# A Strassen-like feed-forward on one core: all pairs of both later parts in seven products, a spare unit before each run of downs, third sums in the fifth group

## The chip, the core and the metric

The kernel runs on one core of a Trainium2 chip, and its time is device microseconds of one execution. TensorE does the matrix products, VectorE, ScalarE and GpSimd do elementwise work, and SyncE issues the loads. Each engine works through its own queue in order and waits on semaphores for operands that another engine makes. Matrix results land in PSUM banks; everything else lives in SBUF. All times below are in microseconds unless marked otherwise.

## The reference, cut to what matters

The reference is a decoder trunk of two layers on 512 tokens of width 1024. Each layer has a half-step feed-forward block, a mixer (convolution and attention) and a second half-step feed-forward block, so there are four feed-forward blocks in a run. Each has 2816 hidden features:

```python
def swiglu(h, w_gate, w_up, w_down):
    return (jax.nn.silu(h @ w_gate) * (h @ w_up)) @ w_down

x = x + 0.5 * swiglu(rms_norm(x, ffn1_norm[l]), ffn1_w_gate[l], ffn1_w_up[l], ffn1_w_down[l])
...
x = x + 0.5 * swiglu(rms_norm(x, ffn2_norm[l]), ffn2_w_gate[l], ffn2_w_up[l], ffn2_w_down[l])
```

The change touches only these four blocks.

## The kernel before, in words

**Three multiplications for one.** Weights and activations are float32. Each operand is split into a high part (a copy rounded by ScalarE) and a low part (what the rounding left, by VectorE), and a product is three matmuls: high by high, high by low, low by high.

**Parts.** The 2816 hidden features are 22 tiles of 128. A feed-forward block takes them in three parts, given by `PARTS` (L45) as first tile, number of tiles, number of pairs: five tiles without pairs, eight tiles in four pairs, nine tiles in three pairs and three tiles over. The first part is done plainly (`ffn`, L703 to L752). The other two are done in units (L378), and this is where the change is.

**Units and the seven products.** A unit computes a 2 by 2 block product by Strassen's scheme in Winograd's form: seven products of half-size blocks instead of eight. A gate/up unit (`GateUp`) computes one hidden tile: the gate and up projections are the two output blocks. Below, g2_0 to g2_7 are the second part's gate/up units and g3_0 to g3_8 the third part's. A down unit (`Down`) computes two of the eight output tiles for all tiles of a part; d2_0 to d2_3 and d3_0 to d3_3 are the second and third part's downs. In a down, two hidden tiles form a pair, and each pair adds one step to each of the seven products; a step is three matmuls with 256 columns. With four steps a product is twelve matmuls, with three it is nine. A tile that is in no pair goes into a down as plain products with 512 columns: two per tile (one for each output tile), six matmuls.

The products are named by their weights and their activations. `u2u1` by `t1`, `g1` by `b11`, `u2` by `t4`, `g2` by `b21`, `all` by `b22`, `g1u2u1` by `t2`, and `g1u1` by `t3`. The last one, the left-over product, is run by the method `rest`, called from the body of the unit that follows. A unit has two PSUM banks, four halves a, d (first bank) and b, c (second bank). `u2u1` by `t1` fills c, `u2` by `t4` goes into d, `g1` by `b11` into a, `g2` by `b21` into b, `all` by `b22` adds to c, and `g1u2u1` by `t2` writes into a again. So the halves are copied away by ScalarE in between: c at L396, a and d at L413, and a (with `t2` in it) at L433. `g1u2u1` by `t2` can't start before the copy of L413, and the left-over product can't start before the copy of L433.

**Weights.** While a unit runs, the next unit's weights are loaded into `wraw` tiles and made ready: GpSimd forms the weight sums (`sums`, L354 to L358), ScalarE the high parts (`hi`, L364), VectorE the low parts (`lo`, L368). There are four pieces: A (`u1`, `u2`, `u2u1`), B (`g1`, `g2`), D (`g1u1`, 512 wide) and C (`g1u2u1`, `all`).

**Hidden activations.** A gate/up unit ends with the addition of L485 and the silu of L486. Its left-over product runs in the next unit's body, followed by L491, L492 and L493, which finish the hidden tile. `Gated.add` then splits it into hh (high, L672) and hl (low, L677). An even tile of a pair is first held in a copy (L657), and its half is subtracted (L662) before the split; these are the activations for `b11`, `t1`, `b21` and `b22`. `b11` and `t1` read the first and the second half of the even tiles, `b21` and `b22` those of the odd tiles. So in a part of eight tiles the last step of `b21` reads the hl of the last tile.

**Sums.** From each pair, `combine` (L679) makes three combinations as soon as its odd tile is finished (for the second part's last pair from `finish`, L497, for the others a unit later, L430). These stand in L685 to L687, and it splits them: the first two together (L690 high, L692 low), which `t2` and `t3` read, and the third sums (L689 high, L691 low), which `t4` reads.

**Order.** `body` (L391) writes down the order within a unit. TensorE's order is fixed by pinning the first matmul of each product (L380). The order on VectorE and ScalarE is the scheduler's (`PIN` is False, L47): it may move an instruction away from where the code has it, by what it expects to be ready first. The order of units is made at L755 to L765. Before the downs of the second part stands one gate/up unit of the third part as a spare, so that the second part's last hidden tile can be finished beside it:

```python
for n in (*range(8, many), *range(min(many, 8)))
...
units += gates[:1] + downs + gates[1:]
```

So the units of a block are g2_0 to g2_7, g3_8, d2_0 to d2_3, g3_0 to g3_7, d3_0 to d3_3. The spare unit makes the ninth, unpaired tile, and d3_0 stands directly behind g3_7, a tile that is unpaired too. In d2_0 alone (`sums_last`, L509) `u2` by `t4` is run in the fourth place, after the left-over product of the gate/up unit; in all other units it is second. In the third part's downs three unpaired tiles go in plainly, by `plain` (L558) and `spare` (L567): the tiles 6 and 7 with weights from B and A, the ninth from D and C (`self.ninth`). In d3_0 they come late (`close`, L593 and L601), in d3_1 and d3_2 early, in d3_3 at the end. `close` adds the kept halves (L594) and adds the results to x (`into`, L581).

## Time and profile before

| | |
|---|---|
| three runs | 1775.48, 1773.82, 1774.02; median 1774.02 |
| the profiled execution | 1775.77, of which the span is 1774.0 |
| granted TensorE clock, mean | 0.999 |
| TensorE busy | 1762.0 (99%), 11869 instructions |
| VectorE busy | 1418.2 (80%), 2021 instructions |
| ScalarE busy | 996.4 (56%), 1591 instructions |
| GpSimd busy | 999.9 (56%), 665 instructions |
| moved by DMA | 177.89 MB, mean 100 GB/s |

The span is the time from the first to the last instruction on the chip. A group row of the profile reads: line, engine, operation, output and inputs by their names in the program, shape, count, then the busy time and the mean in ns of one, then the engine's idle time just before them and what ended most of it. `PEld` is the loading of weights into TensorE, `PE` the matmul itself. A row in order of time reads: start in us from the span's start, duration, engine, line, operation; in brackets the idle time before it and what ended that. In such rows the records of matmuls overlap, so that what a matmul costs is the distance of two starts.

### The profile page before, as it was taken

Reading aid. Unit: us, or ns where it says so; the run is one execution under the profiler, and the core shown is the slowest. Engines: PE = TensorE matmul, PEld = TensorE weight load, DVE = VectorE, ACT = ScalarE, POOL = GpSimd, SP = SyncE. Lnnn points to the kernel's source line nnn. Section 1 sums busy time; section 2 is a strip of 40 time slices with the busy share of each in tenths; the row PEclk is TensorE's granted clock in tenths of the full one; section 3 lists DMA queues with packets and bytes.
Section 4 is the critical chain, followed back from the end, with each engine's and each line's share of the span. In section 5 each row is a group of like instructions: output and inputs, shape, how many; then the busy total and the mean of one; then the engine's idle time right before and its main releaser. Section 6 shows DMA issues by size and latency. Waiting matters only on the chain.

```text
span 1774.0 us, 30565 instructions
## 1 busy us (share of the span) xinstructions
PE 1762.0 (99%) x11869; PEld 1624.0 (92%) x11869; DVE 1418.2 (80%) x2021; ACT 996.4 (56%) x1591; POOL 999.9 (56%) x665
## 2 busy tenths in 40 slices
PE   9999999999999999999999999999999999999999
PEld 7899999988788899999988999999887888999998
DVE  6978878868857978888778788887788588788785
ACT  6456566545844456556534665665558354565663
POOL 3176666369863156766403666653798532567661
PEclk9999999999999999999999999999999999999999
DMA  6232333332122223323332333324231232333332
GB/s 225 91 117 98 108 108 105 124 106 96 36 84 84 84 96 108 108 96 114 112 108 71 103 101 108 108 94 157 71 110 34 72 108 71 108 96 108 108 105 75
DMA packets 74226, 177.89 MB, mean 100 GB/s; under 512 B 8951, under 2 KB 30726, under 8 KB 74080
## 3 DMA queue, kind: packets, MB, share of 16 engines
q1 hardware_dynamic: 72480, 174.10, 29.9%
q8 instruction: 93, 1.52, 0.4%
q0 software_dynamic: 1312, 1.67, 0.3%
q14 instruction: 53, 0.43, 0.1%
q10 hardware_dynamic: 288, 0.16, 0.0%
HBM read 173.79 MB, written 3.42 MB: 100 GB/s over the span
## 4 chain that ended last, share of the span: by engine, by line
PE 84%; DVE 9%; issue 3%; POOL 2%; ACT 1%; DMA 1%; SPq 0%; DVEq 0%; ACTq 0%
PE ps_pair L378 44%; PE ps_pair L142 5%; PE ps_pair L141 5%; PE ps_pair L138 5%; DVE wlo L368 4%; PE ps_d L141 2%; PE ps_d L138 2%; PE ps_d L142 2%; PE ps_sc L1018 2%; PE ps_d L378 2%; PE ps_pair L894 2%; PE ps_pair L896 2%; PE ps_pair L895 2%; PE ps_out L138 1%; PE ps_out L142 1%
## 5 line engine op out<-in xcount | busy, mean ns | idle before, releaser
L368 DVE TENSOR_TENSOR wlo<-wraw,whi 128x1024 fp32r<-128x1024 f32 (+2 forms) x400 | 527.1, 1318 | 152.6 <-ACT whi L364 152.0
L364 ACT ACTIVATE whi<-wraw 128x1024 fp32r<-128x1024 f32 (+2 forms) x400 | 378.1, 948 | 312.1 <-PE ps_pair L378 135.7
L355 POOL TENSOR_TENSOR wraw<-wraw 128x512 f32<-128x512 f32 (+1 forms) x100 | 132.2, 1322 | 518.4 <-DVE wlo L368 315.3
L378 PE MATMUL ps_pair<-acth,wlo 128*128 128x256 f32 x1088 | 307.9, 283 | 0.0
L378 PE MATMUL ps_pair<-actl,whi 128*128 128x256 f32 x1088 | 307.9, 283 | 0.0
L378 PE MATMUL ps_pair<-acth,whi 128*128 128x256 f32 x1088 | 307.9, 283 | 0.0
L378 PE MATMUL ps_pair<-th,whi 128*128 128x256 f32 x816 | 232.1, 284 | 0.8
L378 PE MATMUL ps_pair<-tl,whi 128*128 128x256 f32 x816 | 230.9, 283 | 0.0
L378 PE MATMUL ps_pair<-th,wlo 128*128 128x256 f32 x816 | 230.8, 283 | 0.0
L378 PEld LDWEIGHTS ps_pair<-actl,whi 128*128 128x128 f32 x1088 | 208.9, 192 | 0.2
L378 PEld LDWEIGHTS ps_pair<-acth,whi 128*128 128x128 f32 x1088 | 208.9, 192 | 0.2
L378 PEld LDWEIGHTS ps_pair<-acth,wlo 128*128 128x128 f32 x1088 | 208.9, 192 | 0.0
L101 ACT ACTIVATE whi<-wraw 128x1024 fp32r<-128x1024 f32 (+3 forms) x124 | 122.9, 1001 | 148.9 <-PE ps_pair L141 84.7
L358 POOL TENSOR_TENSOR wraw<-wraw 128x512 f32<-128x512 f32 (+1 forms) x100 | 179.7, 1797 | 7.8
L141 PE MATMUL ps_pair<-actl,whi 128*128 128x512 f32 x448 | 174.8, 391 | 0.3 <-DVE actl L227 0.2
L138 PE MATMUL ps_pair<-acth,whi 128*128 128x512 f32 x448 | 173.9, 393 | 0.6 <-ACT whi L101 0.6
L142 PE MATMUL ps_pair<-acth,wlo 128*128 128x512 f32 x448 | 174.1, 391 | 0.0
L357 POOL TENSOR_TENSOR wraw<-wraw 128x512 f32<-128x512 f32 (+1 forms) x100 | 167.9, 1679 | 7.8
L356 POOL TENSOR_TENSOR wraw<-wraw 128x512 f32<-128x512 f32 (+1 forms) x100 | 166.5, 1665 | 7.6
L378 PEld LDWEIGHTS ps_pair<-th,whi 128*128 128x128 f32 x816 | 156.5, 192 | 2.8 <-ACT keep L433 2.4
L378 PEld LDWEIGHTS ps_pair<-tl,whi 128*128 128x128 f32 x816 | 156.6, 192 | 0.0
L378 PEld LDWEIGHTS ps_pair<-th,wlo 128*128 128x128 f32 x816 | 156.6, 192 | 0.0
(205 smaller groups left out, 4458.6 us busy)
## 6 DMA issues: line engine op xcount, KB each, us to landing
wraw<-in_gu SPq DMA_DIRECT2D x172, 512.0 KB, 3.5
wraw<-in_wqkv SPq DMA_DIRECT2D x24, 512.0 KB, 3.5
wraw<-in_wag SPq DMA_DIRECT2D x16, 512.0 KB, 3.5
wraw<-in_wout SPq DMA_DIRECT2D x16, 512.0 KB, 3.5
wraw<-in_dn SPq DMA_DIRECT2D x60, 128.0 KB, 2.9
wraw<-in_dn SPq DMA_DIRECT2D x20, 384.0 KB, 3.2
wraw<-in_dn SPq DMA_DIRECT2D x28, 256.0 KB, 2.9
wraw<-in_dn SPq DMA_DIRECT2D x20, 320.0 KB, 3.1
```

The source lines that it names most:

```text
L101: S.activation(hi, raw, AF.Copy)
L138: first = T.matmul(ps, wh, xh, start=start, stop=False)
L141: T.matmul(ps, wh, xl, start=False, stop=False)
L142: T.matmul(ps, wl, xh, start=False, stop=stop)
L355: G.tensor_tensor(d, g1, u1, op=ALU.add)
L356: G.tensor_tensor(u1, u1, u2, op=ALU.add)
L357: G.tensor_tensor(m0, u1, g1, op=ALU.add)
L358: G.tensor_tensor(m1, m0, g2, op=ALU.add)
L364: pinned(S.activation(hi[:, : self.cols[k]], self.raw[k][:, : self.cols[k]], AF.Copy), pin)
L368: pinned(V.tensor_tensor(out=lo[:, :c], in0=self.raw[k][:, :c], in1=f32(hi[:, :c]), op=ALU.subtract), pin)
L378: mm = T.matmul(ps, l, r, start=first and i == n == 0, stop=False, skip_group_check=True)
L894: T.matmul(ps[n], xh[:, t], wh, start=k == 0, stop=False)
```

## The change

It has five pieces.

1. `PARTS`: the third part's nine tiles are four pairs and one tile over, where they were three pairs and three over. Each of its downs has four steps per product, and one plain tile.
2. The order of the third part's gate/up units: tile 0 comes first and is the spare unit before d2_0, then 1 to 8. The ninth tile (n = 8) is now the last, and it stands between the last paired tile and d3_0. The third part's pairs are held and finished in other buffers (`hold`, `spot`, `part`), since tile 0 lives through the second part's downs.
3. In the first down of both parts (`q` = 0) a body of its own: `u2` by `t4` moves to the fifth place, after `g2` by `b21`, and the copy of L413 with it. All other units have `t4` second, as before.
4. `combine` makes the combinations and splits the third sums; the split of the other two (L690, L692) moves into `settle`, which is called right after for most pairs, and from the first down's body for the last pair of a part. That last pair is combined from `finish` in both parts (`soon`).
5. The ninth tile's weights for all eight output tiles are loaded once, with d3_0's weights, and split in d3_0 (`part_ninth`, 256 columns and then 768), where each down loaded and split its own two blocks within C and D.

```diff
-PARTS = ((0, 5, 0), (5, 8, 4), (13, 9, 3))
+PARTS = ((0, 5, 0), (5, 8, 4), (13, 9, 4))
...
-            if not self.sums_last:
-                self.go(self.d, "u2", "t4", first=True)
+            self.go(self.d, "u2", "t4", first=True)
...
-            if self.sums_last:
-                self.go(self.a, "g1", "b11", first=True)
             if prev:
                 prev.rest()
-            if self.sums_last:
-                self.go(self.d, "u2", "t4")
-            else:
-                self.go(self.a, "g1", "b11")
+            self.go(self.a, "g1", "b11")
...
-            self.soon = n == 2 * gated.pairs - 1 and n + 1 == gated.many
+            self.soon = n == 2 * gated.pairs - 1
...
         def combine(self):
-            self.gated.combine(self.n, self.banks[0])
+            if self.n % 2:
+                self.gated.combine(self.n, self.banks[0])
+                self.gated.settle()
...
+            self.raw = {"A": u, "B": g, "C": more, "D": d}
+            self.cols = {"A": whole * P, "B": whole * P, "C": 2 * J, "D": J}
+            if self.left and not self.q:
+                self.h.ninth = ring("wraw")
+                for m in range(KT):
+                    pull(self.h.ninth, m * P, m, whole, self.many)
...
+        def body(self, nxt, prev, prev2):
+            if self.q:
+                return super().body(nxt, prev, prev2)
+            if nxt:
+                nxt.load()
+            self.begin()
+            self.go(self.c, "u2u1", "t1", first=True)
+            pinned(S.activation(self.keep[:, 3], self.c, AF.Copy))
+            self.h.settle()
+            nxt.hi("A")
+            nxt.lo("A")
+            self.go(self.a, "g1", "b11", first=True)
+            prev.rest()
+            prev.finish(0)
+            prev.finish(1)
+            nxt.hi("D")
+            nxt.lo("D")
+            prev.finish(2)
+            self.go(self.b, "g2", "b21")
+            self.go(self.d, "u2", "t4")
+            pinned(S.activation(self.keep[:, :2], by_two(self.banks[0]), AF.Copy))
+            nxt.hi("B")
+            self.go(self.c, "all", "b22")
+            nxt.lo("B")
+            nxt.hi("C")
+            self.go(self.a, "g1u2u1", "t2")
+            pinned(S.activation(self.keep[:, 2], self.a, AF.Copy))
+            if self.left:
+                self.h.part_ninth(0, 2)
+            self.close()
+            nxt.lo("C")
+            if self.left:
+                self.h.part_ninth(2, KT)
...
         def plain(self, ps, n, first=False):
...
+            m = 2 * self.q + n
+            w = [tuple(t[:, m * P : (m + 1) * P] for t in self.h.nine)]
+            self.product(ps, zip(w, [self.h.hh[self.many - 1]]), first)
...
+        def part_ninth(self, m0, m1):
+            if not m0:
+                th = self.fp.tile([P, 6, SEQ], F32R, tag="th", name="nine")
+                self.nine = [th[:, 2 * n : 2 * n + 2, :].rearrange("p n c -> p (n c)") for n in range(2)]
+            c = slice(m0 * P, m1 * P)
+            hi, lo = (t[:, c] for t in self.nine)
+            pinned(S.activation(hi, self.ninth[:, c], AF.Copy))
+            pinned(V.tensor_tensor(lo, self.ninth[:, c], f32(hi), op=ALU.subtract))
...
             pinned(S.activation(four[:, a], last, AF.Copy))
-            pinned(S.activation(hi, t, AF.Copy))
             pinned(V.tensor_tensor(four[:, b], last, f32(four[:, a]), op=ALU.subtract))
-            pinned(V.tensor_tensor(lo, t, f32(hi), op=ALU.subtract))
             self.sums.append((hi, lo, four))
+            self.open = t, hi, lo
+
+        def settle(self):
+            if self.open:
+                t, hi, lo = self.open
+                self.open = None
+                pinned(S.activation(hi, t, AF.Copy))
+                pinned(V.tensor_tensor(lo, t, f32(hi), op=ALU.subtract))
...
-                gates = [
-                    GateUp(fp, halves, gu[m0 + n, 0], gu[m0 + n, 1], n, h)
-                    for n in (*range(8, many), *range(min(many, 8)))
-                ]
+                gates = [GateUp(fp, halves, gu[m0 + n, 0], gu[m0 + n, 1], n, h) for n in range(many)]
                 units += gates[:1] + downs + gates[1:]
```

More of the change, by code (lines that the diff above doesn't have):

```diff
@@ L415, in body @@
                 prev.finish(0)
-            if nxt and self.early_free:
+            if nxt:
                 nxt.lo("B")
@@ L572, in early @@
         def early(self):
-            if self.early_free and not self.last:
+            if self.left and not self.last:
                 self.spare()
         def middle(self):
-            if self.early_free and not self.last:
+            if self.left and not self.last:
                 self.plain(self.banks[1], 0)
@@ L587, in close @@
             two, keep = by_two(self.banks[1]), self.keep
-            late = not self.early_free or self.last
-            rest = 2 * self.steps < self.many
+            late = self.left and (self.last or not self.q)
             if self.last:
@@ L618, in rest, with one_tile, __init__, spot @@
             self.after(B)
+    def one_tile(pool, tag, dtype, name, bufs=None):
+        return pool.tile([P, SEQ], dtype, tag=tag, name=name, **({"bufs": bufs} if bufs else {}))
     class Gated:
[L622 to L625 removed]
+        def __init__(self, fp, pairs, many, ahead=False):
+            self.fp, self.pairs, self.many, self.ahead = fp, pairs, many, ahead
+            self.hh, self.sums, self.held, self.slots, self.open = {}, [], {}, [], None
+        def spot(self, n):
+            return (n - 1) % self.many if self.ahead else n
+        def hold(self, n):
+            if self.ahead and not n:
+                return const.tile([P, P + SPACE], F32, tag="ones_r", name="hold")[:, :SEQ]
+            return one_tile(self.fp, ("hh", "hl")[n // 2 % 2] + ("7" if self.ahead else "8"), F32, "hold")
         def part(self):
@@ L655, in add @@
                 if first:
-                    self.held[n] = self.fp.tile([P, SEQ], F32, tag=self.hold[n // 2 % 2], name="hold")
+                    self.held[n] = self.hold(n)
                     pinned(S.activation(self.held[n], us, AF.Copy))
```

65 lines of the change are left out of this document (21 added, 44 removed).

## Prediction

> **What bounds the kernel.** I read the page first (engines, chain), then TensorE's idle time by group, then TensorE, VectorE, ScalarE and GpSimd in order of time around the first down of the second part.
>
> ```profile
> PE 1762.0 (99%) x11869; PEld 1624.0 (92%) x11869; DVE 1418.2 (80%) x2021; ACT 996.4 (56%) x1591; POOL 999.9 (56%) x665
> ...
> PE 84%; DVE 9%; issue 3%; POOL 2%; ACT 1%; DMA 1%; SPq 0%; DVEq 0%; ACTq 0%
> ...
> L378 PEld LDWEIGHTS ps_pair<-th,whi 128*128 128x128 f32 x816 | 156.5, 192 | 2.8 <-ACT keep L433 2.4
> ```
>
> TensorE is busy 99% of the span, so a gain must come from fewer TensorE slots or from the few waits inside its stream. Those are small: 2.4 us in all behind the copy of L433, and, in the groups by shape, 2.5 us behind the third sums (L691):
>
> ```profile
> L378 PEld LDWEIGHTS ps_pair<-hs,whi 128*128 128x128 f32 x672 | 105.9, 192 | 3.5 <-DVE hs L691 2.5
> ```
>
> 2.5 us is four times 0.62: once in each of the four feed-forward blocks. What a slot costs is read from TensorE in order of time, in a last-block down:
>
> ```profile
> 1739.81 0.28 PE L378 MATMUL ps_pair<-hh,whi 128*128 128x256 f32 x1
> ...
> 1741.25 0.40 PE L378 MATMUL ps_pair<-hh,whi 128*128 128x512 f32 x1
> ...
> 1743.32 0.28 PE L378 MATMUL ps_pair<-hh,whi 128*128 128x256 f32 x1
> ```
>
> Twelve 256-wide matmuls start in 1741.25 - 1739.81 = 1.44 us (0.120 each), nine 512-wide in 2.07 us (0.230 each). The records themselves (0.28, 0.40) overlap.
>
> **The place that decides.** Below is the first down of the second part, d2_0, in the first block. Its product groups of twelve start on TensorE at 180.85 (u2u1 by t1), 182.29 (g1 by b11), 183.73 (the gate/up unit's left-over product), 185.17 (u2 by t4, the third sums) and 187.32 (g2 by b21).
>
> ```profile
> 185.17 0.40 PE L378 MATMUL ps_pair<-hs,whi 128*128 128x256 f32 x2
> ...
> 186.25 0.28 PE L378 MATMUL ps_pair<-hs,whi 128*128 128x256 f32 x1
> 186.98 0.39 PE L378 MATMUL ps_pair<-hs,whi 128*128 128x256 f32 x1 [0.44 <-DVE hs L691]
> 187.20 0.28 PE L378 MATMUL ps_pair<-hs,wlo 128*128 128x256 f32 x1
> 187.32 0.28 PE L378 MATMUL ps_pair<-hh,whi 128*128 128x256 f32 x1
> ...
> 190.19 0.28 PE L378 MATMUL ps_pair<-hs,whi 128*128 128x256 f32 x1
> ```
>
> The fourth group's eleventh matmul is due at 186.37 and starts at 186.98, 0.61 late; the next follows after 0.22 instead of 0.12, so such a hold costs 0.10 more: 0.70 in all. VectorE's queue says why:
>
> ```profile
> 180.84 2.32 DVE L368 TENSOR_TENSOR wlo<-wraw,whi 128x1024 fp32r<-128x1024 f32 x1
> ...
> 183.41 1.45 DVE L692 TENSOR_TENSOR hs<-hold,hs 128x512 fp32r<-128x512 f32 x1
> 184.78 1.21 DVE L368 TENSOR_TENSOR wlo<-wraw,whi 128x1024 fp32r<-128x1024 f32 x1
> 185.91 0.69 DVE L485 TENSOR_TENSOR ps_pair<-ps_pair,keep 128x512 f32<-128x512 f32 x1
> 186.51 0.41 DVE L691 TENSOR_TENSOR hs<-ps_pair,hs 128x256 fp32r<-128x256 f32 x1
> 186.84 0.68 DVE L677 TENSOR_TENSOR hl<-ps_pair,hh 128x512 fp32r<-128x512 f32 x1
> 187.44 0.42 DVE L491 TENSOR_TENSOR ps_pair<-ps_pair,keep 128x256 f32<-128x256 f32 x1
> 187.89 0.43 DVE L492 TENSOR_TENSOR ps_pair<-ps_pair,keep 128x256 f32<-128x256 f32 x1
> 188.24 0.68 DVE L368 TENSOR_TENSOR wlo<-wraw,whi 128x512 fp32r<-128x512 f32 x1
> 188.84 0.69 DVE L493 SCALAR_TENSOR_TENSOR ps_pair<-ps_pair,keep 128x512 f32<-128x512 f32 x1
> 189.44 1.94 DVE L368 TENSOR_TENSOR wlo<-wraw,whi 128x1024 fp32r<-128x1024 f32 x1
> 191.29 0.68 DVE L677 TENSOR_TENSOR hl<-ps_pair,hh 128x512 fp32r<-128x512 f32 x1
> 191.90 3.95 DVE L368 TENSOR_TENSOR wlo<-wraw,whi 128x1024 fp32r<-128x1024 f32 x2
> ```
>
> Without a gap come the low half of the sums (L692), two other pieces, the low half of the third sums (L691, done 186.92), and only then the low half of the last feature tile, hl (L677, done 187.52). TensorE starts 0.06 after the operand it lacks (186.92 to 186.98). b21 reads that last tile in its tenth to twelfth matmuls.
>
> **The change, part by part.**
>
> (1) Slots. In each of the third part's four downs one more pair goes into the seven products: twelve 512-wide matmuls go (12 x 0.230 = 2.76), 21 of 256 come (21 x 0.120 = 2.52). Gain 0.24 a down, 0.96 a block, 3.84 in all; the instruction count is settled by the diff. [...] The trace's slots say 3.84.
>
> (2) d2_0, u2 by t4 moved to the fifth place, g2 by b21 to the fourth. The diff means to put the sums' two parts (L690, L692) off until the down has begun. In the built order nothing of that is left: on VectorE and ScalarE the instructions and their waits are the same as before up to L491/L677 of this place, with L692 ahead of L691 and hl behind both. So VectorE's times above stand, and b21, now in the fourth place, asks at 186.37 for an hl that is done at 187.52: start 187.58, hold 1.21 + 0.10 = 1.31, where t4's was 0.70. T4 then finds its operands ready. Cost +0.61 at t2, due 190.80 instead of 190.19.
>
> (3) The copy L413 of the a and d halves now follows t4 in the fifth place, with one group (b22) instead of two until t2 overwrites a. In ScalarE's built order stand before it: the high parts of D and B, a hold copy (the next gate is now the first of a pair) and the high part of C.
>
> ```profile
> 186.63 0.60 ACT L486 ACTIVATE keep<-ps_pair 128x512 f32<-128x512 f32 x1 [1.95 <-DVE ps_pair L485]
> 187.13 1.57 ACT L364 ACTIVATE whi<-wraw 128x512 fp32r<-128x512 f32 x2
> 188.60 0.59 ACT L413 ACTIVATE keep<-ps_pair 128x512 f32<-128x512 f32 x1
> 189.56 0.60 ACT L672 ACTIVATE hh<-ps_pair 128x512 fp32r<-128x512 f32 x1 [0.38 <-DVE ps_pair L493]
> 190.06 1.05 ACT L364 ACTIVATE whi<-wraw 128x1024 fp32r<-128x1024 f32 x1
> ```
>
> Worked out: t4 runs 187.92 to 189.36, and what waits for it is released 0.22 later (last start + 0.28 + 0.06), at 189.58. The hold copy waits for L493 (189.53): 189.58 to 190.18. C's high part, 1.05: to 191.15. L413, 0.59: 191.05 to 191.64 (starts overlap by 0.1, as in the rows). t2 starts at 191.70, due 190.80: 0.90 + 0.10 = 1.00. Bounds: 0, if the copy were served right at 189.58 (190.17); 1.6, if a transfer or a sum is late by one more 0.6 copy. I take 1.00, the queue as built. d2_0 in sum: +1.61 a block.
>
> (4) The third part's gates in order 0 to 8, with n = 8 as the spare unit before d3_0, and a fourth pair. The new pair adds per block five ScalarE and eight VectorE instructions (with those of the ninth tile's weights). In the gate units they lie beside TensorE: the second part's gates do the same work with no hold but the L433 ones, which I leave as they are. But d3_0 now meets what d2_0 meets. Before it had three unpaired tiles and slack, VectorE waiting 3.00 us in its middle:
>
> ```profile
> 313.11 0.70 DVE L594 TENSOR_TENSOR ps_pair<-ps_pair,keep 128x512 f32<-128x512 f32 x1 [3.00 <-PE ps_pair L378]
> ```
>
> After the change the built order around d3_0 is that of d2_0 (L692, a weight part, L485, L691, hl), so on d2_0's clock: b21 waits for hl, +1.31 (bounds 0, if VectorE is 1.15 ahead here, and 1.7 with one more piece of 0.4 before hl).
>
> (5) d3_0's L413 stands behind two copies of the ninth tile's weights (256 and 768 wide), B, C and hh:
>
> ```profile
> L318 ACT ACTIVATE th<-ht 128x768 fp32r<-128x768 f32 x16 | 13.1, 837 | 2.3 <-DVE ht L317 2.2
> L689 ACT ACTIVATE hs<-ps_pair 128x256 fp32r<-128x256 f32 x28 | 10.7, 382 | 9.5 <-DVE ps_pair L687 9.5
> ```
>
> 187.75 + 0.38 + 0.84 less overlaps = 188.8; B to 189.8; C to 190.7; hh to 191.2; L413 to 191.72; t2 191.78, due 190.80: 0.98 + 0.10 = 1.08 (bounds as in 3).
>
> (6) d3_0's plain product follows t2. Its second matmul (due 191.78 + 1.44 + 0.10 + 0.23 = 193.55) needs hl of the ninth tile, and VectorE's built order puts before that: L491, L492, D (188.92 as above), the ninth's weights 256 wide, L493, the ninth's 768 wide, B and C.
>
> ```profile
> L319 DVE TENSOR_TENSOR tl<-ht,th 128x768 fp32r<-128x768 f32 x16 | 15.0, 950 | 0.0
> 189.00 1.29 POOL L355 TENSOR_TENSOR wraw<-wraw 128x512 f32<-128x512 f32 x1 [4.69 <-DVE wlo L368]
> 190.37 2.15 POOL L356 TENSOR_TENSOR wraw<-wraw 128x512 f32<-128x512 f32 x1
> 192.60 2.16 POOL L357 TENSOR_TENSOR wraw<-wraw 128x512 f32<-128x512 f32 x1
> ```
>
> 188.9 + 0.4 (L691's size) + 0.65 + 0.95 = 190.9; B 1.94 and C 1.97 (half of 3.95): 194.75; hl 0.6: 195.35; TensorE at 195.41: hold 1.86 + 0.10 = 1.96. The weight parts take 1.94 and 1.97 instead of 1.21 where GpSimd's sums run (rows of 189.00 on), and the same sums run here. Bounds: 0.3 with 1.21 for each; 3.6 with 2.32 for each and the ninth's parts slowed as well. I take the rows of the same stretch. [...]
>
> (7) At nothing:
>
> ```profile
> wraw<-in_dn SPq DMA_DIRECT2D x60, 128.0 KB, 2.9
> ```
>
> GpSimd's sums are 512 instead of 384 wide, by the rows of 189.00 on a quarter of 1.29 + 3 x 2.15, 1.9 more a down; cover: GpSimd is 56% busy. C is 1024 wide instead of 896, an eighth of 1.21, 0.15 more on VectorE. The ninth tile's eight loads stand in SyncE's queue ahead of d3_1's, no longer with each down; one lands 2.9 after its issue, and the unit they lie beside lasts 84 x 0.120 = 10.1. Uncovered, they would cost up to 2.9 a block. Queued behind the held matmuls is all of TensorE's stream, so holds add in full.
>
> **Sum.** Per block -0.96 + 1.61 + 1.31 + 1.08 + 1.96 = +5.00; four blocks +20.0. The profiled execution took 1775.77 (span 1774.0): 1795.8. The median shown is 1774.02, 1.75 lower: I predict 1794.0. What a measurement of this kernel tells from no change is about 0.2%, 3.5 us.
>
> **Rivals.**
> - It gets faster: the fifth place hides t4 and no other hold comes. Per block -0.96 - 0.70, so 1767.4. It decides if hl is done before 186.37, that is if VectorE has 1.15 less before it there. For it: t4 alone was late. Against: L677's row behind L691. 5%.
> - d2_0 as worked out, d3_0 without any hold, because VectorE enters the third part's gates rested: -0.96 + 1.61 = +0.65, 1776.6, no change to be told. It needs VectorE over 1.15 ahead at d3_0. Against: nine units lie between, as before d2_0. 7%.
> - Only the b21 holds: ScalarE serves L413 in time and hl of the ninth is nearly hidden: -0.96 + 0.61 + 1.31 + 0.3 = +1.26, 1779.1 (up to 1784 with one hold more). 15%.
> - All holds as worked out, between 1784 and 1803: 63%.
> - VectorE's backlog after d3_0 also reaches d3_1, or the shifted loads come late: above 1803 (1.96 raised to 3.6 gives 1800.6; loads 2.9 late in each block 1805.6). 10%.
>
> Range 1779 to 1803. Faster by over 0.2% 0.05, within 0.07, slower 0.88.
>
> **What would show it.** TensorE's group on hh and hl idle behind L677's successor, about 1.2 in d2_0 and in d3_0 of each block; the third-sum wait (L691) gone from TensorE; waits on the copy of a and d before t2, about 1; a wait of 2 on hl in d3_0's 512-wide group; 512-wide matmuls of L378 down by 192, 256-wide up by 336. I am wrong if VectorE's hl comes ahead of L692, if d3_0 starts with VectorE idle, or if the ninth tile's hl is early.

## The result, and the profile after

The changed kernel takes 1805.12 (median of six, 1802.98 to 1806.43), the kernel before, measured beside it, 1774.78 (1773.82 to 1777.25). The ratio is 1.0169, 95% interval 1.0156 to 1.0182. The profiled execution took 1805.85, its span 1803.7, 29.7 longer than the span before. The forecast was 1794.0 with a range up to 1803.0: the direction and most places were right, the time lies 2.1 above the range, and the rise is half as large again as the forecast one.

The page of the changed kernel, parts 1 and 6; a row of part 6 ends with the median us from issue to landing:

```profile
PE 1765.9 (98%) x12013; PEld 1630.7 (90%) x12013; DVE 1458.7 (81%) x2053; ACT 1007.2 (56%) x1611; POOL 1032.8 (57%) x665
...
wraw<-in_dn SPq DMA_DIRECT2D x60, 128.0 KB, 3.2
```

TensorE lost its 99%. Where it waits is in its groups by shape; the last field is the idle time ahead of the group and what ended it:

```profile
L378 PE MATMUL ps_pair<-hl,whi 128*128 128x256 f32 x512 | 146.1, 285 | 7.4 <-DVE hl L716 7.4
...
L378 PE MATMUL ps_pair<-hs,whi 128*128 128x256 f32 x704 | 132.5, 287 | 5.9 <-ACT keep L564 5.9
...
L378 PE MATMUL ps_pair<-hh,nine 128*128 128x512 f32 x32 | 13.9, 436 | 5.6 <-DVE ps_pair L608 5.6
...
L378 PE MATMUL ps_pair<-hl,nine 128*128 128x512 f32 x16 | 7.2, 450 | 8.7 <-DVE hl L716 8.7
```

Three of these are the forecast ones: b21 for hl (7.4), t2 for the copy of a and d (5.9; L564 is the copy's line in the first downs), the ninth tile's plain product for its hl (8.7). The wait on the third sums' low half (L691 before) is gone. The third row, 5.6 behind the addition of L608, was in no step of the prediction.

TensorE in order of time in block 1, at the first four of these places:

```profile
187.35 0.39 PE L378 MATMUL ps_pair<-hl,whi 128*128 128x256 f32 x1 [1.02 <-DVE hl L716]
...
191.41 0.50 PE L378 MATMUL ps_pair<-hs,whi 128*128 128x256 f32 x2 [0.70 <-ACT keep L564]
...
310.72 0.39 PE L378 MATMUL ps_pair<-hl,whi 128*128 128x256 f32 x1 [0.88 <-DVE hl L716]
...
318.95 0.50 PE L378 MATMUL ps_pair<-hl,nine 128*128 128x512 f32 x1 [2.17 <-DVE hl L716]
```

The brackets count from the modelled end of the matmul before. By the distance of starts, less the slot, the holds are 1.18, 0.86, 1.04 and 2.33 (and 0.93 at 314.85 for d3_0's copy), each with about 0.10 more at the next matmul. These are the numbers used below.

At the end of the last down, d3_3, there is a place that the prediction passed over:

```profile
354.64 0.40 PE L378 MATMUL ps_d<-hh,nine 128*128 128x512 f32 x1
...
355.11 0.39 PE L378 MATMUL ps_d<-hh,nine 128*128 128x512 f32 x1
358.03 0.80 PE L378 MATMUL ps_pair<-hh,nine 128*128 128x512 f32 x1 [2.52 <-DVE ps_pair L608]
358.62 0.63 PE L378 MATMUL ps_pair<-hl,nine 128*128 128x512 f32 x1
```

The spare product is down to three matmuls, and the next one waits for the addition of L608 (L594 before): 358.03 - 355.11 - 0.23 = 2.69. VectorE and ScalarE there, after the change:

```profile
355.54 0.70 DVE L617 TENSOR_TENSOR ps_d<-ps_d,keep 128x512 f32<-128x512 f32 x1 [0.77 <-PE ps_d L378]
356.15 1.22 DVE L102 TENSOR_TENSOR wlo<-wraw,whi 128x1024 fp32r<-128x1024 f32 x1
357.28 0.69 DVE L608 TENSOR_TENSOR ps_pair<-ps_pair,keep 128x512 f32<-128x512 f32 x1
...
354.77 1.06 ACT L101 ACTIVATE whi<-wraw 128x1024 fp32r<-128x1024 f32 x1 [1.57 <-issue]
355.74 0.36 ACT L427 ACTIVATE keep<-ps_pair 128x256 f32<-128x256 f32 x1
```

Two things are seen. The copy of a (L427) stands behind a weight part of the mixer that follows (L101). And on VectorE the spare product's subtraction and another mixer weight part (L102, 1.22) stand ahead of the addition. Before, the same place had nine spare matmuls, 2.07, in front of the addition, which came early enough:

```profile
346.00 0.38 ACT L433 ACTIVATE keep<-ps_pair 128x256 f32<-128x256 f32 x1 [1.08 <-PE ps_pair L378]
...
346.41 0.70 DVE L594 TENSOR_TENSOR ps_pair<-ps_pair,keep 128x512 f32<-128x512 f32 x1 [1.13 <-ACT keep L433]
```

Behind two kinds of hold the matmuls themselves are slow. Windows of the changed kernel; the columns are stretch, length, busy time of TensorE, its weight loads, VectorE, ScalarE and GpSimd with their instructions, granted TensorE clock, DMA share and GB/s:

```profile
317.00:319.00 2.00, 0.05 (x1) 0.06 (x1) 2.00 (x3) 1.33 (x2) 1.92 (x2) 1.00 0.74 242
...
320.50:323.80 3.30, 3.30 (x17) 3.30 (x17) 2.39 (x4) 0.38 (x1) 1.14 (x1) 0.50 0.21 78
324.00:327.00 3.00, 3.00 (x25) 2.86 (x24) 1.25 (x2) 2.35 (x4) 0.00 (x0) 1.00 0.02 5
...
358.00:361.40 3.40, 3.37 (x13) 3.09 (x14) 1.46 (x3) 0.96 (x2) 0.00 (x0) 0.51 0.48 154
```

For 3.413 after some of the long holds the granted clock is 0.50: from 320.37 on, 1.4 after d3_0's hold has ended in block 1, and from 357.92 on, just before d3_3's ends. A 256-wide matmul then takes 0.213 instead of 0.120, a 512-wide one 0.43. In this execution such a stretch stands behind d3_0's hold in block 1 and behind d3_3's in blocks 1 and 3, and costs 1.45, 1.59 and 1.42. Blocks 2 to 4 have the same hold of 2.33 or 2.34 at d3_0 with no slow stretch; the fifth experiment comes back to this.

The account of the 29.7, from starts on TensorE:

| | forecast | in the trace |
|---|---|---|
| slots | -3.84 | -3.7 |
| d2_0: b21 and t2, less t4's old wait | +6.4 | +6.2 |
| d3_0: b21 | +5.2 | +4.4 |
| d3_0: t2 | +4.3 | +4.1 |
| d3_0: plain product | +7.8 | +9.8 |
| d3_3: plain product | none | +6.2 |
| matmuls at half the clock | none | +4.5 |
| outside the units (most of it in the first mixer) | none | -1.6 |

The slots' row is what is left of the four blocks' growth (10.94, 5.17, 9.33, 5.94) when the rows under it down to the clock's are taken off; it is 0.89 to 0.98 a block. The last row is not the change's: the profiled execution of the kernel before has a stretch at clock 0.50 in its first mixer, from 494.92 on, and that of the changed kernel has none there.

### The profile page after: what moved, and what is told of

It reads as the page before. It is cut to its first block, busy times and chain, and to the rows that moved or that the text cites. A ratio compares the mean times of both kernels' runs of the same rounds, so it can differ in the third digit from the quotient of the medians.

```text
span 1803.7 us, 30881 instructions
## 1 busy us (share of the span) xinstructions
PE 1765.9 (98%) x12013; PEld 1630.7 (90%) x12013; DVE 1458.7 (81%) x2053; ACT 1007.2 (56%) x1611; POOL 1032.8 (57%) x665
## 3 DMA queue, kind: packets, MB, share of 16 engines
q8 instruction: 94, 1.54, 0.4%
## 5 line engine op out<-in xcount | busy, mean ns | idle before, releaser
L368 DVE TENSOR_TENSOR wlo<-wraw,whi 128x1024 fp32r<-128x1024 f32 (+1 forms) x400 | 549.9, 1376 | 146.3 <-ACT whi L364 145.8
L364 ACT ACTIVATE whi<-wraw 128x1024 fp32r<-128x1024 f32 (+1 forms) x400 | 380.2, 952 | 298.4 <-PE ps_pair L378 145.0
L355 POOL TENSOR_TENSOR wraw<-wraw 128x512 f32<-128x512 f32 x100 | 137.0, 1370 | 517.6 <-DVE wlo L368 290.7
L378 PE MATMUL ps_pair<-actl,whi 128*128 128x256 f32 x1120 | 317.0, 283 | 0.0
L378 PE MATMUL ps_pair<-acth,wlo 128*128 128x256 f32 x1120 | 316.9, 283 | 0.0
L378 PE MATMUL ps_pair<-acth,whi 128*128 128x256 f32 x1120 | 316.9, 283 | 0.0
L378 PEld LDWEIGHTS ps_pair<-acth,whi 128*128 128x128 f32 x1120 | 215.1, 192 | 0.2
L378 PEld LDWEIGHTS ps_pair<-actl,whi 128*128 128x128 f32 x1120 | 215.0, 192 | 0.2
L378 PEld LDWEIGHTS ps_pair<-acth,wlo 128*128 128x128 f32 x1120 | 215.0, 192 | 0.0
L101 ACT ACTIVATE whi<-wraw 128x1024 fp32r<-128x1024 f32 (+3 forms) x124 | 123.2, 1000 | 153.2 <-PE ps_pair L141 91.9
L358 POOL TENSOR_TENSOR wraw<-wraw 128x512 f32<-128x512 f32 x100 | 186.8, 1868 | 7.8
L357 POOL TENSOR_TENSOR wraw<-wraw 128x512 f32<-128x512 f32 x100 | 178.9, 1789 | 7.8
L356 POOL TENSOR_TENSOR wraw<-wraw 128x512 f32<-128x512 f32 x100 | 173.5, 1735 | 7.6
```

The costliest lines, as they stand in the source:

```text
L101: S.activation(hi, raw, AF.Copy)
L355: G.tensor_tensor(d, g1, u1, op=ALU.add)
L356: G.tensor_tensor(u1, u1, u2, op=ALU.add)
L357: G.tensor_tensor(m0, u1, g1, op=ALU.add)
L358: G.tensor_tensor(m1, m0, g2, op=ALU.add)
L364: pinned(S.activation(hi[:, : self.cols[k]], self.raw[k][:, : self.cols[k]], AF.Copy), pin)
```

## The experiments

Each is an edit of the changed kernel unless it says otherwise; `pin` keeps an instruction behind the one that the code has ahead of it on its engine. The kernel before was measured again beside them, with medians from 1774.05 to 1775.36, so the times alone don't tell differences of 1 or 2 between experiments.

**The last down's plain products early.** The argument `last` is false for d3_3 too.

```diff
-                    Down(fp, dn, m0, many, pairs, q, h, after if end else lambda m: None, end and q == KT // 2 - 1)
+                    Down(fp, dn, m0, many, pairs, q, h, after if end else lambda m: None, False)
```

> One edit to the changed kernel: the last down of the third part (d3_3) runs its two plain products early, like d3_1 and d3_2, and no longer behind the addition of L608 at its end. The changed kernel is 1805.1; its trace shows TensorE idle 2.69 at that place in blocks 1 and 3 (0.68 in block 4), and after the first two some 1.5 each of matmuls at about twice their slot. Theory A (the hold is the place's own: three matmuls of the spare product are too short a cover for the copy of a and the addition): the idle and the slow stretch go, -2 x 4.2 - 0.8 = -9.2, so 1796. Theory B (VectorE and ScalarE are late there anyway, with the next phase's weights in front): the next phase's first products wait instead, and 1803 to 1806 stays.

Measured: 1802.87, ratio to the kernel before 1.0164 (1.0149 to 1.0179): not to be told from the changed kernel. The wait on L608 is gone, and another stands a little further on:

```profile
L378 PE MATMUL ps_pair<-hs,whi 128*128 128x256 f32 x704 | 131.1, 284 | 9.1 <-ACT keep L564 5.9 <-ACT keep L427 3.2
```

The unit's own left-over product writes into a, so it waits for the copy of a (L427): 1.51 in blocks 1 and 3, 0.63 in block 4. Theory B had the place wrong (not the next phase's products) and the reason right: the copy itself is late, behind the mixer's weights. In block 4, where no mixer follows, the copy starts at once and the product still waits 0.63, because nothing stands between t2 and it. So the lateness of the copy is 1.51 - 0.63 = 0.88 of d3_3's 2.69.

**Hl ahead of the sums.**

```diff
-            self.h.settle()
+            self.h.settle(True)
...
-                pinned(S.activation(hi, t, AF.Copy))
-                pinned(V.tensor_tensor(lo, t, f32(hi), op=ALU.subtract))
+                pinned(S.activation(hi, t, AF.Copy), pin)
+                pinned(V.tensor_tensor(lo, t, f32(hi), op=ALU.subtract), pin)
```

> One edit to the changed kernel: in both first downs the split of the last pair's sums is held behind the copy of L551 (pinned in program order), so that VectorE makes the low half of the last paired tile (hl, L716) ahead of the sums' low half (L738, 1.45). Theory A (holds are single and add up): the waits on hl in d2_0 (1.18 + 0.10) and d3_0 (1.04 + 0.10) go, -4 x 2.42 = -9.7, so 1795.4. Theory B (VectorE's backlog is the limit, and the same work still stands ahead of the copies that t2 waits for): the wait on hl goes, but the copy of a and d (L564) comes at the same time as before, so that the wait at t2 grows by 0.5 to 1.2 in each; in d3_0 the plain product's wait on the ninth tile's hl grows by what is left. Then -2 to -5 in all, so 1800 to 1803.

Measured: 1796.84, 1.0124 (1.0107 to 1.0141), so 8.3 less: nearer to A. VectorE around d2_0:

```profile
182.12 1.98 DVE L368 TENSOR_TENSOR wlo<-wraw,whi 128x1024 fp32r<-128x1024 f32 x1
184.03 0.69 DVE L476 TENSOR_TENSOR ps_pair<-ps_pair,keep 128x512 f32<-128x512 f32 x1
184.62 0.41 DVE L729 TENSOR_TENSOR hs<-ps_pair,hs 128x256 fp32r<-128x256 f32 x1
184.96 0.68 DVE L716 TENSOR_TENSOR hl<-ps_pair,hh 128x512 fp32r<-128x512 f32 x1
185.56 0.68 DVE L738 TENSOR_TENSOR hs<-hold,hs 128x512 fp32r<-128x512 f32 x1
```

Hl stands ahead of the sums' low half (L738) and b21's hold is 0.11 in block 1, about 0.6 in the other three; at d3_0 it is gone. The copy's holds did not grow as B had it: 0.79 in d2_0 and 0.32 in d3_0. The ninth tile's wait stayed at 2.1 to 2.5. So the order was the cause of b21's wait in d3_0, and of half of it or more in d2_0: there the weight part that moved up in front of hl takes 1.98, where it took 1.21, and eats part of the 1.45. The waits are mostly single ones.

**The copy of a and d ahead of B and C.** In the first downs' body:

```diff
-            nxt.hi("B")
+            nxt.hi("B", True)
...
-            nxt.hi("C")
+            nxt.hi("C", True)
```

> One edit to the changed kernel: in both first downs the next down's high parts B and C are held behind the copy of a and d (L564) on ScalarE, which then follows at once on the weight part D (and, in d2_0, the hold copy). Theory A (holds add up): the waits on that copy before t2 go, 0.96 in d2_0 and 1.03 in d3_0, -8.0 in all, so 1797. Theory B (VectorE's backlog is the limit): in d2_0 the wait goes (-3.8), but in d3_0 the plain product then waits for the ninth tile's hl by as much more, so 1801.

Measured: 1795.21, 1.0115 (1.0100 to 1.0131), more than A. In d2_0 the wait is gone, in d3_0 0.26 is left of 0.93. But the edit did a second thing: with the high parts B and C later, the scheduler put their low parts behind the ninth tile's hl, and that wait (2.33) went too. In return copies in the next downs come late: d2_1's left-over product waits 0.43 for the copy of a, and d3_1's t2 0.78 for that of a and d in blocks 2 and 3. Neither theory had that; as a test of the copy alone the run is spoilt.

**The ninth tile's hl ahead of D, B and C in d3_0.**

```diff
-            nxt.hi("D")
-            nxt.lo("D")
+            nxt.hi("D", bool(self.left))
+            nxt.lo("D", bool(self.left))
...
-            nxt.lo("B")
+            nxt.lo("B", bool(self.left))
```

> One edit to the changed kernel: in d3_0 the ninth tile's hl (L716) stands ahead of the next down's low parts D, B and C on VectorE (pinned in program order), as hh does ahead of the high part D on ScalarE. My reading (1.94 + 1.97 of low parts B and C stand in front of hl): the plain product's wait of 2.33 + 0.11 goes, and the stretch of slow matmuls behind it in block 1 with it: -4 x 2.44 - 1.5 = -11.3, so 1794. Rival (the low parts are then late for d3_1, whose u2u1 by t1 and g1 by b11 wait for them): the wait is passed on to d3_1, 1800 to 1805.

Measured: 1797.10, 1.0126 (1.0111 to 1.0141), 8.0 less. The wait on the ninth tile's hl is gone in all four blocks, and d3_1 doesn't wait for its weights: the rival falls. In the trace t2's wait in d3_0 went down too, from 0.93 to 0.32, 2.5 in all that the forecast did not have. What is missing came back in other places. D3_3's hold is now 3.61 in blocks 1 and 3, with slow matmuls behind both (mean granted clock 0.996), 3.3 more: TensorE came earlier to a place where the addition comes when it comes. B21's wait in d3_0 is longer in blocks 2 to 4, 1.6 more in all; it varies from trace to trace (1.56 in block 4 of the last experiment, which leaves this place as it is). And this execution has a slow stretch in its first mixer, 1.6.

**TensorE kept busy in d3_3's hold.** `fills` is [1, 0, 1, 0], one entry for each block.

```diff
             if self.last:
                 self.spare()
+                if fills.pop(0):
+                    self.fill()
...
+        def fill(self):
+            ps = bank(("y", "tp")[self.q % 2], "ps_fill")
+            for n in range(11):
+                mm = T.matmul(ps, self.h.nine[0][:, :P], self.h.hh[8][0], start=n == 0, stop=False, skip_group_check=True)
+                tc.keep_in_program_order(mm)
```

> One addition to the changed kernel: in d3_3 of blocks 1 and 3, TensorE runs eleven more 512-wide matmuls into a bank that nobody reads, between the spare product and the one that waits for the addition of L608 (11 x 0.230 = 2.5, the hold there is 2.69). Theory A (the slow matmuls behind a long hold come from TensorE having been idle): the hold's end stays where it is, the matmuls behind it start at 0.230 and 0.120 again, and the time falls by the slow stretches of these two places, about 1.4 each where an execution has them: 1802 to 1804. Theory B (the slow stretch has another cause than the idle time): slots of about 0.43 and 0.21 stand behind the filled hold too, and 1805 stays.

Measured: 1803.50, 1.0157 (1.0140 to 1.0174). The times alone don't separate the two, the trace does. The windows of the filled place in block 1, and the matmuls behind it:

```profile
352.50:357.00 4.50, 4.48 (x26) 3.57 (x24) 3.73 (x5) 1.33 (x2) 0.16 (x1) 1.00 0.36 122
357.00:360.40 3.40, 3.40 (x21) 3.05 (x22) 2.19 (x4) 1.49 (x3) 0.59 (x5) 1.00 0.63 172
```

```profile
357.00 0.50 PE L380 MATMUL ps_pair<-hh,nine 128*128 128x512 f32 x1
357.33 0.40 PE L380 MATMUL ps_pair<-hl,nine 128*128 128x512 f32 x1
357.57 0.39 PE L380 MATMUL ps_pair<-hh,nine 128*128 128x512 f32 x1
357.80 0.40 PE L380 MATMUL ps_pair<-hs,whi 128*128 128x256 f32 x2
```

The granted clock is 1.00 and the slots are 0.23, in both filled places. So here the slow stretch follows the idle time, not the place.

Whether a hold is followed by one can be compared within the changed kernel's trace. Its slow stretches in the units last 3.413 each and start whole multiples of 3.413 apart: at 320.37, 357.92 and 1252.21, which lie 11 and 262 times 3.413 from one to the next. So this trace can be cut into stretches of 3.413 on its own grid. Four of them; a slow one follows the first three, none the fourth:

```profile
316.96:320.37 3.41, 1.42 (x7) 1.21 (x8) 3.41 (x3) 1.33 (x2) 3.25 (x3) 1.00 0.71 219
354.51:357.92 3.41, 0.99 (x6) 0.52 (x4) 2.64 (x5) 1.33 (x2) 0.00 (x0) 1.00 0.51 155
1248.80:1252.21 3.41, 1.29 (x8) 0.81 (x7) 2.65 (x4) 1.33 (x2) 0.00 (x0) 1.00 0.47 151
1211.25:1214.66 3.41, 1.59 (x13) 1.27 (x11) 3.41 (x3) 1.33 (x2) 3.33 (x2) 1.00 0.32 99
```

By the distances of starts less the slots, TensorE is idle for 2.10, 2.58, 2.29 and 1.99 in these. In the units of this trace every other stretch at full clock has 1.76 or less, and none of those is followed by a slow one. The holds of 2.33 and 2.34 in blocks 2 to 4 lie across a border of the grid (the one that ends at 1215.02 across 1214.66), and the stretch that has most of such a hold has 1.75, 1.99 and 1.76 of idle time in all. How many slow stretches an execution has differs between executions of one kernel: the mean granted clock of the changed kernel's six is 0.997 to 0.999.

**D2_0 back in its old order.** A body of its own for the second part's first down, with t4 behind the left-over product and b21 behind t4.

```diff
+            if not self.left:
+                return self.body2(nxt, prev, prev2)
...
+            self.go(self.a, "g1", "b11", first=True)
+            prev.rest()
+            self.go(self.d, "u2", "t4")
+            pinned(S.activation(self.keep[:, :2], by_two(self.banks[0]), AF.Copy))
...
+            self.go(self.b, "g2", "b21")
+            nxt.hi("C")
+            self.go(self.c, "all", "b22")
+            self.go(self.a, "g1u2u1", "t2")
```

> One part of the change undone: d2_0 alone has the order of the kernel before (t4 in the fourth place, b21 in the fifth, the copy of a and d behind them); everything else is as in the changed kernel. By the prediction's steps (2) and (3), with what the trace of the changed kernel shows: b21's wait (1.18 + 0.10) and t2's wait (0.86 + 0.10) go, t4's wait of 0.70 comes back, 4 x -1.54 = -6.2, so 1799. Rival (the waits come from the work that the new order of gates brings, not from the moved product): d2_0 keeps about 2.2 of waiting and 1804 to 1806 stays.

Measured: 1801.64, 1.0151 (1.0136 to 1.0166), 3.5 less. In the trace b21's and t2's waits are gone from d2_0, and t4's is back at 0.58 in blocks 2 to 4:

```profile
L378 PE MATMUL ps_pair<-hs,whi 128*128 128x256 f32 x704 | 132.1, 285 | 4.4 <-ACT keep L566 3.1 <-DVE hs L758 1.3
```

The waits of d2_0 belong to the moved product; the rival falls. The gain is less than 6.2 in part because this profile has slow matmuls in five places, with a mean granted clock of 0.995 (three and 0.997 in the changed kernel's).

**The code's order everywhere.**

```diff
-PIN = False
+PIN = True
```

> The changed kernel with PIN = True: VectorE and ScalarE keep the order in which the code has the units' instructions (hl ahead of the sums' low half, the copy of a and d ahead of the high part B, the sums in the first down's body as written). Theory A (the order that the scheduler chose makes the holds of the first downs): b21's, t2's and the plain product's waits go in d2_0 and d3_0, -4 x 6.85 = -27.4 at best, so 1778, and 1785 with one of them left. Theory B (VectorE has too much to do before these places in any order, and a fixed order lets other instructions wait in line): holds of the same sum stand elsewhere, 1795 or more.

Measured: 1917.83, 1.0804 (1.0788 to 1.0820). Theory B, and far beyond it:

```profile
L378 PE MATMUL ps_pair<-th,whi 128*128 128x256 f32 x816 | 241.6, 296 | 52.6 <-DVE hs L729 52.6
...
L378 PE MATMUL ps_pair<-hs,whi 128*128 128x256 f32 x704 | 138.0, 294 | 30.2 <-ACT keep L564 23.4 <-ACT keep L407 6.8
```

In the code's order the gate/up units wait for the third sums' low half of the pair just combined (L729), whose source lies in the unit's bank. The scheduler's freedom is worth far more than the places that it spoils.

**Three pins and d3_3 reordered.** The edits of "Hl ahead of the sums", "The copy ahead of B and C" and "The ninth tile's hl" together, and t2 ahead of b22 in the last down:

```diff
-            self.go(self.c, "all", "b22")
+            if nxt:
+                self.go(self.c, "all", "b22")
             self.go(self.a, "g1u2u1", "t2")
             pinned(S.activation(self.keep[:, 2], self.a, AF.Copy))
+            if not nxt:
+                self.go(self.c, "all", "b22")
```

> The changed kernel with three orders pinned in both first downs (the sums' split behind the copy of L551; the high parts B and C behind the copy of a and d; in d3_0 the ninth tile's hl ahead of the low parts D and B), and with t2 ahead of b22 in d3_3, so that twelve more matmuls cover the copy and the addition there. If the holds are single ones and add up, 6.85 - 0.7 (b21 in d2_0 stayed at 0.6 when its order alone was pinned) = 6.1 a block goes, -24.6, and in d3_3 about 1.2 in two blocks and the slow stretches, -6: 1775, the time of the kernel before. If VectorE's backlog passes them on (to d3_1's copies and to d3_3), 1783 to 1790.

Measured: 1782.67, 1.0042 (1.0027 to 1.0057), so 22.5 of the 30 are gone. That lies 7.7 above the first forecast and just below the second's range: most holds were single, and part was passed on. No slow matmuls are left in the trace's feed-forward blocks (mean granted clock 1.000), and the executions lie within 1.1 of each other where the changed kernel's lie within 3.5. What is left: 0.58 and 0.52 in d2_0, 0.36 and 0.50 in d3_0, 0.82 in d3_2 of three blocks (the copy of a and d, L407; the changed kernel has no hold there), 1.32 in d3_3 of two.

**One step of the change alone, on the kernel before.** The split of the second part's last sums pinned late, all else as before.

```diff
             pinned(S.activation(four[:, a], last, AF.Copy))
-            pinned(S.activation(hi, t, AF.Copy))
             pinned(V.tensor_tensor(four[:, b], last, f32(four[:, a]), op=ALU.subtract))
-            pinned(V.tensor_tensor(lo, t, f32(hi), op=ALU.subtract))
             self.sums.append((hi, lo, four))
+            self.open = t, hi, lo
+            if n + 1 < self.many:
+                self.settle()
...
             pinned(S.activation(self.keep[:, 3], self.c, AF.Copy))
+            if self.sums_last:
+                self.h.settle(True)
```

> The kernel before (three pairs, its order of units, t4 in the fourth place of d2_0) with one step of the change alone, and made to hold: the split of the second part's last sums is pinned behind the copy of L396 in d2_0, so that the third sums' low half (L691) and hl come 1.45 earlier on VectorE. By my reading of the first trace (L692, 1.45, stands ahead of L691, which is 0.61 late) the wait of 0.70 in each block goes: -2.8, so 1772 where the kernel before has 1774.5. Rival (another piece takes its place on VectorE, or t2 then waits for the sums): within 1 of the kernel before.

Measured: 1772.67 over eleven runs against 1774.11 over sixteen, ratio 0.9991, interval 0.9982 to 1.0000. VectorE at d2_0:

```profile
185.09 0.41 DVE L692 TENSOR_TENSOR hs<-ps_pair,hs 128x256 fp32r<-128x256 f32 x1
185.42 0.68 DVE L679 TENSOR_TENSOR hl<-ps_pair,hh 128x512 fp32r<-128x512 f32 x1
186.02 0.68 DVE L701 TENSOR_TENSOR hs<-hold,hs 128x512 fp32r<-128x512 f32 x1
```

All four waits of t4 are gone, and the four blocks' units are shorter by 0.56 to 0.59 each, 2.3 in all. In the medians 1.4 of it is seen, at the edge of what the measurement tells. Slow stretches in the mixers blur the times: the profiled execution of this kernel has two, from 493.54 and 1374.18 on (mean granted clock 0.998), that of the kernel before one (0.999). Among the executions whose mean granted clock was 1.000, this kernel took 1771.21 to 1771.88 (four) and the kernel before 1773.29 to 1774.30 (eight). It has the lowest median of this study.

**The combined kernel with d2_0 in the old order, sums late.** The three pins and d3_3's order as two experiments above, with the body that puts d2_0 back in its old order, and `settle(True)` in that too.

> The last combined kernel (1782.7) with d2_0 back in the order of the kernel before, the sums' split pinned late as there. In its trace d2_0 still had 0.58 + 0.52 + 0.20 of waiting a block. Theory A (the moved product gains nothing over the old order once the sums are late): 4 x -1.3 = -5.2, so 1777.5. Theory B (b21 or t2 waits for hl or the copy in the old order too): 1780 to 1783.

Measured: 1780.59, 1.0035 (1.0022 to 1.0048), so 2.1 less where 5.2 was expected. By the ratios it is 1.2 and the intervals overlap, so the times don't tell the two apart; the profiled spans differ by 2.9. In the trace the holds of d2_0 (1.3 a block) are gone but for 0.09, and d2_1's left-over product now waits 0.29 + 0.10 for its copy of a. That leaves about 0.8 a block. The time lies in theory B's range, but b21 and t2 don't wait: it is theory A for d2_0, with a part passed on to the next unit.

**The ninth tile's second weight piece later.** As the last, and `part_ninth(2, KT)` pinned.

```diff
-                self.h.part_ninth(2, KT)
+                self.h.part_ninth(2, KT, True)
```

> As the kernel before it in this call, and the second piece of the ninth tile's weights (768 columns) pinned behind the low part C in d3_0 on ScalarE and VectorE, so that hh and hl of the ninth tile come 0.84 and 0.95 earlier. If these pieces are what is left of the wait at d3_0's plain product (0.36 + 0.50 + 0.2 a block): -4.2 more, so 1773. If d3_1's spare product, which reads that piece, now waits for it instead: no gain, 1777 or more.

Measured: 1792.97, 1.0108 (1.0095 to 1.0122), 12 more. The wait moved on and grew:

```profile
L378 PE MATMUL ps_d<-hh,nine 128*128 128x512 f32 x32 | 14.0, 437 | 12.6 <-ACT nine L709 8.6 <-DVE nine L710 4.0
```

D3_1's spare product now waits 3.0 and then 1.3 for this piece in blocks 1 to 3, with slow matmuls behind (mean granted clock 0.995). D3_0's waits are gone, as expected, but this place is worse for the piece.

**T2 ahead of b22 in d3_3 alone.** The diff shown with the three pins, without the pins.

> The changed kernel with t2 ahead of b22 in d3_3 alone. If the hold there (2.69 in blocks 1 and 3, 0.68 in block 4) comes from a cover that shrank from nine 512-wide matmuls to three (2.07 to 0.69) in front of an addition whose operand comes late, 1.44 more of cover takes 1.2 to 1.4 off each of the two long ones, and with a hold of 1.3 the slow stretch behind it does not come: 1800 to 1803. If the addition is late by itself (its copy and the next phase's weights on ScalarE and VectorE come when they come), the hold stays above 2.

Measured: 1797.44, a single run, below the forecast. The hold is 0.33 in blocks 1, 3 and 4, where 1.3 was expected to be left. The trace has no slow stretch in its feed-forward blocks (mean granted clock 1.000), not even behind d3_0's hold of 2.34 in block 1, which the edit leaves as it is; that 1.45 is not the edit's. D3_3 in block 1:

```profile
354.00 0.39 PE L378 MATMUL ps_d<-hh,nine 128*128 128x512 f32 x1
354.56 0.50 PE L378 MATMUL ps_pair<-hh,nine 128*128 128x512 f32 x1 [0.17 <-DVE ps_pair L611]
...
352.30 0.38 ACT L428 ACTIVATE keep<-ps_pair 128x256 f32<-128x256 f32 x1 [0.20 <-PE ps_pair L378]
...
353.80 0.70 DVE L611 TENSOR_TENSOR ps_pair<-ps_pair,keep 128x512 f32<-128x512 f32 x1
```

The addition (L611 here) is done by 354.5, where TensorE needs it at 354.23. It is more than the cover: with t2 earlier, the copy (L428) also comes ahead of the second mixer weight, and the addition ahead of the spare product's subtraction. So cover and order are not told apart in blocks 1 and 3. Block 4, with no mixer behind, tells the cover: its hold in the changed kernel is 0.68. The cover shrank by six matmuls, 6 x 0.230 = 1.38, and the slack before was 0.75 (in block 4 the addition was done at 1765.33 + 0.70 and the product that needs it began at 1766.78, in block 1 at 346.41 + 0.70 and 347.86), which leaves 0.63. The other 2.0 in blocks 1 and 3 are what stands ahead of copy and addition: 0.88 by the copy behind the mixer's weight part (L101, first experiment), and 1.12 by the addition behind L617 and L102, which starts 1.54 after the copy (355.74 to 357.28) where it starts 0.42 after it in block 4 (1796.25 to 1796.67). With that order the six matmuls would have covered 1.38 of the 2.69.

## Why the prediction was wrong in size, and where it was right

**Right: the mechanism and the places.** TensorE's stream decides; the sums that the code puts off are back in front of hl in the built order; and the five terms that were costed came to 20.8 in the trace against 20.0 forecast, in part by luck, because d3_0's first two holds were 1.0 shorter in all and its last 2.0 longer. When one of them was taken away, the next hold of the same down did not grow (hl ahead of the sums); what was passed on came mostly in later units, above all in d3_3 (the ninth tile's hl: 2.69 to 3.61).

**(1) Slots.** -3.84 forecast, -3.7 in the trace. The trace's slots, 0.120 and 0.230, were the right price.

**(2), (3) D2_0.** Holds of 1.21 and 0.90 forecast, 1.18 and 0.86 measured. That L564 stands behind the hold copy and the high part C was read from the built order and was so. D2_0 in its old order took both away again.

**(4), (5) D3_0 on d2_0's clock.** 1.21 and 0.98 forecast, 0.93 to 1.04 and 0.93 measured. The rival "d3_0 without any hold because VectorE is rested" fell.

**(6) The plain product.** 1.86 forecast, 2.33 to 2.34 measured. The order was right, a size was off: the low parts B and C took 4.51 for the two, not 1.94 + 1.97, and GpSimd's sums ran beside them (three from 313.31 to 319.42):

```profile
313.78 4.51 DVE L368 TENSOR_TENSOR wlo<-wraw,whi 128x1024 fp32r<-128x1024 f32 x2
318.21 0.68 DVE L716 TENSOR_TENSOR hl<-ps_pair,hh 128x512 fp32r<-128x512 f32 x1
```

2.25 each is near the upper bound's price (2.32).

**What failed: step (1) as an all-gain, and the cover that it took away.** The prediction counted twelve 512-wide matmuls a down as gone and asked nowhere what they had covered. In d3_3 six of them stood between t2 and the product that waits for the addition of L594. Asking there what the prediction asked of the first downs (what waits, and what stands in front of it) would have shown it: the built order has L617 and L102 ahead of L608. That is +6.2 of the missing 9.7: in blocks 1 and 3, 0.67 of the 2.69 is the lost cover itself and 2.0 the order of copy and addition, which the prediction did not read there; in block 4 it is the cover alone.

**What failed: "holds add in full".** They added more than in full at three of the long ones: the slow matmuls behind holds of 2.33 to 2.69 cost 4.5 in the profiled execution. How many such stretches an execution has differs, so this part of the miss varies: the mean granted clock of the six executions is 0.997 to 0.999. The rival above 1803 named another mechanism (late loads, a backlog into d3_1), and neither was seen: d3_1 of the changed kernel has no hold above 0.2.

## What to carry to other kernels

A matmul that a change saves may have been the cover of a wait: for each removed group ask what starts behind it and how long that had been done. Where the code says that a step comes later, read it in the built order of that engine, and pin the one instruction that matters, not all of them: one pin on the kernel before took 2.3 of waiting away, all pins on the changed kernel cost 113. And keep TensorE's holds short: here three of 2.33 to 2.69 cost another 1.42 to 1.59 each, in matmuls at half the clock.

## What the runs showed of the hardware that was not expected

In the changed kernel's trace the granted TensorE clock fell to 0.50 for 3.413 after holds of 2.33 to 2.69, but not after each: 2.33 and 2.34 in blocks 2 to 4 were not followed by it. The slow stretches lie on a grid of 3.413: in the units of this trace the three stretches of the grid with 2.10, 2.29 and 2.58 of idle time were followed by a slow one, and those with 1.99 or less were not. With TensorE kept busy through the hold (fifth experiment, 357.00 to 360.40) the clock stayed at 1.00.

The low half of the sums (128x512) took 1.45 where it stood in the changed kernel (L738 at 183.18) and 0.68 when it was made some 2.4 later (second experiment, 185.56), while the weight part that took its place went from 1.21 to 1.98. In the changed kernel's trace the 1.45 began beside a sum of GpSimd (181.91 to 184.07), and the 1.21 (184.55 to 185.76) ran beside none. So the same VectorE piece differed by a factor of 2.1 and 1.6 with its place; that GpSimd's sums are the cause was not tested by itself.
